# A two-layer hybrid decoder step: where products with an inverse deviation, a norm's parts and a scan's steps are emitted

## The chip, the cores and the metric

The kernel runs on one core of one Trainium2 chip, as one launch. The metric is device time in microseconds (us), lower is better; the value that counts is the median over several runs. The kernel before took 1984.57 us, the median of three runs (1982.0 to 1985.96).

The engines are TensorE (PE in the profile: matmuls, with PEld for its weight loads), VectorE (DVE, `V` in the code), ScalarE (ACT, `S`), GpSimd (POOL, `G`) and SyncE (SP, `nc.sync`), which here only issues DMAs.

## The reference

One inference step of a decoder with two layers, for a prompt of 512 tokens and 8 samples of 4 tokens (544 tokens in all, model width 1024). Per layer:

```
h = RMSNorm(x) * (1 + scale1(c)) + shift1(c)
z = h @ W_in
A: causal pooling          B: retention (4 heads), o * rsqrt(mean(o^2) + eps) * silu(gate)
C: short gated convolution D: RWKV-7, a delta-rule state, y normalised per head, bonus, output gate
mixed = sum over branches of sigmoid(gate) * (branch @ w_br);  x = x + gate1(c) * (mixed @ W_out)
h2 = RMSNorm(x) * (1 + scale2(c)) + shift2(c)
x = x + gate2(c) * W_down(silu(a) * b),   [a|b] = causal_dwconv3(h2 @ W_up)
```

A final RMSNorm gives y; each branch also returns its new state. Everything is float32.

## The kernel before, in words

**Layout and matmuls.** Activations lie transposed: channels on 128 partitions, the 544 tokens along the free dimension, split into two halves of 272 (`HS`). Every large product is done in three passes (`mm3`, L156 to L167): weight and activation are each split into a high part (rounded to float32r) and a low part (the rest), and PE runs high x high (L164), high x low (L165) and low x high (L166). `unit` (L200) does one 128-wide output tile for one half: 8 `mm3`, 24 matmuls, into one PSUM tile `pd` (three of them). Another engine evicts it. Weights come by SP's DMA; ACT rounds the high part (`whi`, L130) and DVE subtracts the low part (`wlo`, L134).

**The order is written out.** PE, DVE, ACT and POOL run their instructions in the order in which the Python code emits them; only SP's DMAs are left to a scheduler. So an instruction that waits holds up all that was emitted after it on its engine. Side work is woven between the large matmuls by a clock of matmuls: `nmm[0]` goes up by 3 in each `mm3`, which then calls `slot()` (L183). `later(n, fn)` runs `fn` once n more matmuls were emitted; a generator that was handed to `spawn` yields the number of matmuls until its next step (the sign sets the order in a slot; a `True` behind it lets another generator's matmuls go with that step). `finish(e)` runs all steps that are left at once.

**The mixer.** After eight units for branch D, `rwkv` (L459) is spawned. Meanwhile the main program does the short convolution (6 units), its gates, the pooling (2 units), its gates, the retention's 8 units, then the gates of branch D and of branch B. `gates` (L1210) does per tile of 128 channels a gate unit in both halves, which ACT's sigmoid evicts (L1247), and, one tile later, the projection (2 x 6 matmuls), evicted by DVE with a product (L1227); then POOL (L1229), in the last call DVE, adds it up. In the calls for D and B, `finish` of the generator stands behind the second gate unit.

`rwkv` makes decays and, tile of 128 tokens by tile, `products` (L528): four DVE products that go into `LG` (L544, L546), then four into `bks` (L552) and one into `bkd` (L558), which the matmuls L579 and L586 of the next step read. Then come a substitution of 31 steps on DVE, the scan of 16 chunks (G matmul L734, its copy L696, S matmul L701, its copy L705, state and output matmuls L754 and L758, state update L767 or, in the first chunk, L769), a last chunk for the samples, and a norm: Ln (L450) and Exp (L453) on ACT give the inverse deviation, with which DVE multiplies (L853 and on). `retentions` (L960) waits for the scan's end and then does `retention` for two head pairs: three steps of matmuls, Ln and Exp, and the products L954 and L955, with the split L456 (ACT) and L457 (DVE).

**The norms.** `both_halves` (L384) drives the output projection and the last part of the down projection: 8 tiles for the first half of the tokens, then 8 for the second. DVE adds each tile to x (`residual`, L408 to L415), ACT squares it (L322), DVE adds up the squares (L325). Behind each half a norm generator is spawned: a matmul with ones (L331), square root (L333), reciprocal (L355), then per tile a product (L361, DVE), scale and shift (L338, ACT, with L343 and L344 on DVE for the samples), the high part (L366, ACT) and the low part (L369, DVE). The first half's norm runs beside the second half's tiles; the second half's norm runs beside the first units of the next stage. The last norm, `norm_final`, multiplies on DVE (L379) and sends each pair of tiles out from SP's queue (L381).

Of the kernel before, what the change touches and what calls it, by code (L numbers as in the profile page):

```python
# [12 lines left out]
AF = mybir.ActivationFunctionType  # L13
ALU = mybir.AluOpType
MUL, ADD, SUB, MAX = ALU.mult, ALU.add, ALU.subtract, ALU.max
# [7 lines left out]
PAST_LEN = 4096  # L23
D_FF = 2816
NU = 138
D_G, D_S, D_P = 15, 15, 18
KAPPA = -math.exp(-0.5)

RW_UNITS = [22, 23, 18, 19, 16, 17, 20, 21]
# [14 lines left out]
def tile_hybrid_step(ctx: ExitStack, tc: tile.TileContext, io: dict):  # L44
    nc = tc.nc
    V, S, G, PE = nc.vector, nc.scalar, nc.gpsimd, nc.tensor
# [20 lines left out]
    def ZR(n=562, dt=F32):  # L67
        return zrp.tile([128, n], dt, tag="zr", name=nm("zr"))
# [109 lines left out]
    def later(n, fn):  # L178
        laters.append((nmm[0] + n, fn))
# [136 lines left out]
    def xk(xt, k):  # L316
        return xt[k // 4][:, k % 4, :]

    def sum_sq(acc, x):

        sq = ZR(x.shape[1])
        S.activation(sq, x, AF.Square)  # L322
        if acc is None:
            return sq
        later(5, lambda: V.tensor_tensor(out=acc, in0=acc, in1=sq, op=ADD))  # L325
        return acc

    def rstd_sqrt(acc):
# [21 lines left out]
    def norm_half(xt, half, acc, sA, shA, hh):  # L350

        c0, c1 = HS[half]
        rs = rstd_sqrt(acc)
        yield -8
        V.reciprocal(rs, rs)  # L355
        yield -10
        us = {}
        for i in range(11):
            if i < 8:
                us[i] = ZR(HALF)  # L360
                V.tensor_tensor(out=us[i], in0=xk(xt, i)[:, c0:c1], in1=rs, op=MUL)  # L361
            if 0 <= i - 1 < 8:
                mod_samples(us[i - 1], i - 1, half, sA, shA)
                mod_prompt(us[i - 1], i - 1, half, sA, shA)
            if 0 <= i - 2 < 8:
                S.copy(hilo_of(i - 2, half, hh)[0], us[i - 2])  # L366
            if 0 <= i - 3:
                hi, lo = hilo_of(i - 3, half, hh)
                V.tensor_tensor(out=lo, in0=us[i - 3], in1=hi, op=SUB)  # L369
            yield -8 if half == 0 else -7  # L370

    def norm_final(xt, half, acc):
        c0, c1 = HS[half]
        rs = rstd_sqrt(acc)
        V.reciprocal(rs, rs)
        yield -6
        for k in range(8):
            x = xk(xt, k)[:, c0:c1]
            V.scalar_tensor_tensor(out=x, in0=x, scalar=pars[0][:, P_FG + k:P_FG + k + 1], in1=rs, op0=MUL, op1=MUL)  # L379
            if k % 2:  # L380
                nc.sync.dma_start(io["o_y"][:, k - 1:k + 1, c0:c1], xt[k // 4][:, k % 4 - 1:k % 4 + 1, c0:c1])  # L381
            yield -6

    def both_halves(run, norm):  # L384

        ng = None
        for half in range(2):
            acc = None
            for m in range(8):
                acc = sum_sq(acc, run(m, half))  # L390
                fill()
            if ng:
                finish(ng)
            ng = spawn(norm(half, acc), 24, first=False)
        return ng
# [56 lines left out]
    def exp_half(out):  # L452
        S.activation(out[:, 0:TOK], out[:, 0:TOK], AF.Exp, scale=-0.5)  # L453
# [5 lines left out]
    def rwkv(l, za, zb, M, yD):  # L459
# [68 lines left out]
        def products(T, e1):  # L528
# [8 lines left out]
            for q in range(2):  # L537
                r = par_rows(q)
                o = LG[q][r, 4 * T:4 * T + nch, :, :]
                ot = o.rearrange("r c p t -> r p c t")  # L540
                kb = kkb[r, 0:2, t0:t0 + n].rearrange("r p (c t) -> r p c t", t=32)
                Er = E[r].rearrange("r p (c t) -> r p c t", t=32)
                oa, orr = ot[:, :, :, a_cols(q)], ot[:, :, :, r_cols(q)]
                V.tensor_tensor(out=oa[:, :, :, 1:32], in0=kb[:, :, :, 1:32], in1=Er[:, :, :, 0:31], op=MUL)  # L544
                G.tensor_copy(oa[:, :, :, 0:32:st], kb[:, :, :, 0:32:st])
                V.tensor_tensor(out=orr, in0=zb[r, 0:2, t0:t0 + n].rearrange("r p (c t) -> r p c t", t=32),  # L546
                                in1=Er, op=MUL)
            bks = ZR(512)
            bkv = bks[:, 0:4 * n].rearrange("p (q c w t) -> p q c w t", q=2, w=2, t=32)
            for w, src in enumerate((kkb, za)):  # L550
# [10 lines left out]

        e1 = decays(0)
        yield -16
        bkn = products(0, e1)
        yield 54, True
        for T in range(5):
            n = 128 if T < 4 else 32
            nch = n // 32
# [32 lines left out]
                                          LG[q][b_rows(q, p), 0:16, p, a_cols(q)])  # L601
            if T < 4:
                yield -14
                bkn = products(T + 1, e1)
                yield 50, True
        rks = []
        for p in range(2):
            rk = ZR(TOK)
# [50 lines left out]
        for s in range(31):  # L659
            substitute(s)  # L660
            if s % 2:
                yield -18, False, s > 28
        for h in range(2):
            nc.sync.dma_start(scr2[:, :, h, :], X[64 * h:64 * h + 64])
        for q in range(2):
# [180 lines left out]
            ln_bones(rs, TOK, 1.0 / 64, EPSL, rs)  # L846
        for rs in rss:
            exp_half(rs)
        yield -8
        yD.append(T4(F32R))  # L850
        for p in range(2):
            y = yv[:, p, :]
# [9 lines left out]
    def retention(l, p, rt, M, yB):  # L862
# [19 lines left out]
        for ps in pss:  # L882
# [1 line left out]
            V.tensor_tensor(out=sm.rearrange("j (T i) -> j T i", T=4), in0=ps.rearrange("j (T i) -> j T i", T=4),  # L884
                            in1=cst[:, C_RETM:C_RETM + 128].unsqueeze(1).broadcast_to([128, 4, 128]), op=MUL)
            sms.append(sm)
        yield 36, True
        ps = PM()
        pv = PM()
        for q in range(2):  # L890
# [17 lines left out]
        for T in range(1, 4):  # L908
# [4 lines left out]
        V.tensor_tensor(out=Vx[0:64].rearrange("r (b e) -> r b e", b=NB),  # L913
                        in0=vks[0:64, 0:64].unsqueeze(1).broadcast_to([64, NB, 64]),
                        in1=cst[0:64, C_BM:C_BM + 8].unsqueeze(2).broadcast_to([64, NB, 64]), op=MUL)
        yield 36, True
        psO = PM()
        for T in range(4):
            for q in range(2):
# [31 lines left out]
        rs = ZR(TOK)  # L951
        ln_bones(sq, TOK, 1.0 / 64, EPS6, rs)
        exp_half(rs)
        V.tensor_tensor(out=o, in0=o, in1=rs, op=MUL)  # L954
        V.tensor_tensor(out=o, in0=o, in1=rt[:, 3, :], op=MUL)  # L955
        if p == 0:
# [744 lines left out]
```

## Time and profile before

| | us |
|---|---|
| median of three runs | 1984.57 |
| lowest, highest | 1982.0, 1985.96 |
| the profiled execution | 1986.48 |
| its span on the core | 1984.7 |
| PE busy | 1914.8 |
| DVE busy | 1097.5 |
| ACT busy | 813.6 |
| POOL busy | 244.9 |
| mean granted clock of PE | 0.989 |

How to read the rows of the profile. A row of the order of time is "start, duration (us), engine, line, operation, output<-inputs, shape, xcount", and in brackets how long the engine sat idle before it and what ended that. A row of the list of waits is "who <- for whom: us in all, times, the longest". A row of the groups ends in "busy us, mean ns | idle us before"; a row of one source line has the shortest, median and longest duration in ns. Large matmuls overlap: a duration of 0.29 us is the time through the array, the step from one start to the next is what they cost. A row of stages gives the stretch, its length, the busy time (and number of instructions) of PE, PEld, DVE, ACT and POOL, and then PE's mean granted clock, the DMA engines' busy share and GB/s.

### The profile page before, as it was taken

The page shows a single profiled execution, that of the slowest core. Times are in us where ns is not written, and L with a number is a line of the kernel's source. Part 1 is how long each engine was busy: PE and PEld are TensorE (multiplying, and loading weights), DVE is VectorE, ACT ScalarE, POOL GpSimd, SP SyncE. Part 2 cuts the span into 40 slices and gives each one's busy share as a digit, 9 for nine tenths or more (in the row PEclk, how much of TensorE's full clock was granted, in tenths as well). Part 3 has the DMA queues.
Part 4 walks back from the last instruction along what each step waited for, and adds up shares of the span by engine and source line. Part 5 has one row for each costly group of instructions (what it writes and reads, how often), then busy time and mean ns, then how long its engine had stood idle before and what let it go on. Part 6 is the DMA issues. An engine that isn't in the chain of part 4 may idle for free.

```text
span 1984.7 us, 39086 instructions
## 1 busy us (share of the span) xinstructions
PE 1914.8 (96%) x16188; PEld 1837.4 (93%) x16188; DVE 1097.5 (55%) x2245; ACT 813.6 (41%) x1578; POOL 244.9 (12%) x687
## 2 busy tenths in 40 slices
PE   6999999989999999999989999999899999999997
PEld 5999999888999998899989999998799999999996
DVE  5475755443566552455664756555336765445565
ACT  5643323343345531434355433334424555243532
POOL 1100135311000000000101001451110000000000
PEclk9999999999999999999999999999899999999998
DMA  8223435412334268522332133242124222222221
GB/s 320 87 93 111 121 128 173 147 61 75 131 104 160 86 224 307 193 92 88 115 120 70 64 97 89 65 134 81 59 86 151 83 86 86 86 87 95 86 94 46
DMA packets 75042, 227.15 MB, mean 114 GB/s; under 512 B 20208, under 2 KB 23072, under 8 KB 73072
## 3 DMA queue, kind: packets, MB, share of 16 engines
q1 hardware_dynamic: 69872, 210.43, 31.5%
q0 software_dynamic: 4560, 13.76, 2.2%
q8 instruction: 127, 2.08, 0.4%
q10 hardware_dynamic: 432, 0.46, 0.1%
q14 instruction: 51, 0.42, 0.1%
HBM read 213.33 MB, written 9.06 MB: 112 GB/s over the span
## 4 chain that ended last, share of the span: by engine, by line
PE 88%; DVE 7%; ACT 3%; issue 1%; DMA 0%; POOL 0%; DVEq 0%; SPq 0%; ACTq 0%
PE pd L164 27%; PE pd L166 26%; PE pd L165 26%; PE pm L282 2%; DVE wlo L134 1%; PE pm L734 1%; DVE zr L325 1%; PE pm L754 1%; DVE zr L1227 1%; ACT L453 1%; PE pm L758 1%; PE pm L579 0%; PE pm L586 0%; ACT zr L322 0%; ACT zr L450 0%
## 5 line engine op out<-in xcount | busy, mean ns | idle before, releaser
L164 PE MATMUL pd<-t,whi 128*128 128x272 f32 x4104 | 1210.5, 295 | 23.7 <-DVE zr L1227 20.9
L166 PE MATMUL pd<-t,wlo 128*128 128x272 f32 x4104 | 1192.2, 291 | 2.6 <-DVE wlo L134 2.1
L165 PE MATMUL pd<-t,whi 128*128 128x272 f32 x4104 | 1186.6, 289 | 2.1 <-DVE t L369 1.7
L164 PEld LDWEIGHTS pd<-t,whi 128*128 128x128 f32 x4104 | 778.4, 190 | 57.6 <-DVE zr L1227 24.4
L165 PEld LDWEIGHTS pd<-t,whi 128*128 128x128 f32 x4104 | 780.4, 190 | 4.2 <-DVE t L369 2.1
L166 PEld LDWEIGHTS pd<-t,wlo 128*128 128x128 f32 x4104 | 778.7, 190 | 3.2 <-DVE wlo L134 2.4
L134 DVE TENSOR_TENSOR wlo<-raw,whi 128x1024 fp32r<-128x1024 f32 x256 | 320.7, 1253 | 299.6 <-ACT whi L130 297.2
L130 ACT CAST whi<-raw 128x1024 fp32r<-128x1024 f32 x258 | 270.6, 1051 | 146.6 <-PE pd L165 139.2
L1395 ACT COPY zr<-pd 128x272 f32<-128x272 f32 (+2 forms) x264 | 73.5, 314 | 241.1 <-PE pd L166 241.0
L1247 ACT ACTIVATE zr<-pd 128x272 f32<-128x272 f32 x128 | 50.6, 397 | 215.8 <-PE pd L166 215.4
L408 DVE SCALAR_TENSOR_TENSOR t<-pd,mod,t 128x272 f32<-128x272 f32 (+1 forms) x160 | 76.7, 480 | 85.8 <-PE pd L166 85.4
L1397 POOL COPY off<-zr 128x18 f32<-128x18 f32 x88 | 19.9, 226 | 645.6 <-ACT zr L1395 645.6
L1227 DVE TENSOR_TENSOR zr<-pd,zr 128x272 f32<-128x272 f32 x96 | 40.7, 436 | 79.1 <-PE pd L166 78.6
L1152 DVE SCALAR_TENSOR_TENSOR zr<-zr,par,zr 128x560 f32<-128x560 f32 x92 | 73.8, 802 | 3.2
L1151 DVE SCALAR_TENSOR_TENSOR zr<-zr,par,zr 128x560 f32<-128x560 f32 x92 | 73.2, 796 | 3.7 <-ACT zr L1148 3.6
L1229 POOL TENSOR_TENSOR t<-t,zr 128x272 f32<-128x272 f32 x64 | 57.2, 907 | 142.4 <-DVE zr L1227 136.8
L322 ACT ACTIVATE zr<-t 128x272 f32<-128x272 f32 (+1 forms) x72 | 32.4, 455 | 95.6 <-DVE t L408 55.7
L1148 ACT ACTIVATE zr<-zr,par 128x560 f32<-128x560 f32 x92 | 65.7, 766 | 10.4 <-DVE zr L1177 10.4
L164 PE MATMUL pd<-t,t 128*128 128x272 f32 x224 | 64.8, 289 | 3.4 <-DVE zs L412 3.4
L166 PE MATMUL pd<-t,t 128*128 128x272 f32 x224 | 64.5, 288 | 0.0
L165 PE MATMUL pd<-t,t 128*128 128x272 f32 x224 | 64.4, 287 | 0.0
L696 DVE COPY gs<-pm 32x64 f32<-32x64 f32 x68 | 15.2, 224 | 64.7 <-ACT gs L696 64.1
(285 smaller groups left out, 1778.3 us busy)
## 6 DMA issues: line engine op xcount, KB each, us to landing
raw<-in_wst SPq DMA_DIRECT2D x276, 512.0 KB, 3.4
t<-in_wada SPq DMA_DIRECT2D x32, 1024.0 KB, 9.1
raw<-in_wada SPq DMA_DIRECT2D x24, 512.0 KB, 3.6
zr<-in_rope POOLq DMA_DIRECT2D x16, 272.0 KB, 4.2
t<-in_wada SPq DMA_DIRECT2D x8, 512.0 KB, 6.8
t<-in_xT SPq DMA_DIRECT2D x4, 544.0 KB, 6.2
zr<-zr POOLq DMA_DIRECT2D x32, 68.0 KB, 2.0
t<-in_xT SPq DMA_DIRECT2D x2, 1088.0 KB, 8.9
```

What stands on the lines that cost most here:

```text
L130: S.copy(hi, raw)
L134: (G if (l, u) in ((0, 1), (0, 2)) else V).tensor_tensor(out=lo, in0=raw, in1=hi, op=SUB)
L164: PE.matmul(ps, lhsT=a, rhs=xh, start=first, stop=False)
L165: PE.matmul(ps, lhsT=a, rhs=xl, start=False, stop=False)
L166: PE.matmul(ps, lhsT=b, rhs=xh, start=False, stop=last)
L408: V.scalar_tensor_tensor(out=x[:, c0:c0 + npc], in0=ps[:, :npc], scalar=gate[:, m, 0:1], in1=x[:, c0:c0 + npc], op0=MUL, op1=ADD)
L1148: S.activation(cv, u[:, 0:560], AF.Copy, scale=wcol(0))
L1151: V.scalar_tensor_tensor(out=cv, in0=u[:, 1:561], scalar=wcol(1), in1=cv, op0=MUL, op1=ADD)
L1152: V.scalar_tensor_tensor(out=cv, in0=u[:, 2:562], scalar=wcol(2), in1=cv, op0=MUL, op1=ADD)
L1227: V.tensor_tensor(out=a[:, c0:c1] if first else gs, in0=pp[:, :HALF], in1=gs, op=MUL)
L1229: (V if last else G).tensor_tensor(out=a[:, c0:c1], in0=a[:, c0:c1], in1=gs, op=ADD)
L1395: pad_evac(lambda o, i, sl: S.copy(o, i), u, ps, half, 2)
```

## The change

- The state products of a tile come in two pieces: a yield stands between the `LG` products and the `bks` products, and the yields behind them are shorter.
- The scan's third yield in each chunk (`D_P`) goes from 18 to 15; the substitution's from 18 to 16.
- Between Exp and the products with the inverse deviation stand 24 instead of 8 matmuls in `rwkv`, and 30 instead of none in `retention`. Two yields of `retention` grow from 36 to 46 and 50.
- In the second half of `both_halves`, the sums of squares of the tiles 1 to 5 go to GpSimd (the first tile has no sum, the last two stay on DVE). In the first half's norm, the low parts go to GpSimd. The yields of the norm become 9 (8 before) and 6 (7 before).
- In the last norm, two of eight tiles are scaled by ACT and multiplied by GpSimd. Each tile gets a DMA of its own, on ACT's queue and SP's in turn.

```diff
-D_G, D_S, D_P = 15, 15, 18
+D_G, D_S, D_P = 15, 15, 15
...
-    def sum_sq(acc, x):
+    def sum_sq(acc, x, eng=V):
...
-        later(5, lambda: V.tensor_tensor(out=acc, in0=acc, in1=sq, op=ADD))
+        later(5, lambda: eng.tensor_tensor(out=acc, in0=acc, in1=sq, op=ADD))
...
-                V.tensor_tensor(out=lo, in0=us[i - 3], in1=hi, op=SUB)
-            yield -8 if half == 0 else -7
+                (V if half else G).tensor_tensor(out=lo, in0=us[i - 3], in1=hi, op=SUB)
+            yield -9 if half == 0 else -6
...
-            V.scalar_tensor_tensor(out=x, in0=x, scalar=pars[0][:, P_FG + k:P_FG + k + 1], in1=rs, op0=MUL, op1=MUL)
-            if k % 2:
-                nc.sync.dma_start(io["o_y"][:, k - 1:k + 1, c0:c1], xt[k // 4][:, k % 4 - 1:k % 4 + 1, c0:c1])
+            if k % 4 == 3:
+                S.activation(x, x, AF.Copy, scale=pars[0][:, P_FG + k:P_FG + k + 1])
+                G.tensor_tensor(out=x, in0=x, in1=rs, op=MUL)
+            else:
+                V.scalar_tensor_tensor(out=x, in0=x, scalar=pars[0][:, P_FG + k:P_FG + k + 1], in1=rs, op0=MUL, op1=MUL)
+            (nc.sync if k % 2 else S).dma_start(io["o_y"][:, k:k + 1, c0:c1], xt[k // 4][:, k % 4:k % 4 + 1, c0:c1])
...
-                acc = sum_sq(acc, run(m, half))
+                acc = sum_sq(acc, run(m, half), G if half and m < 6 else V)
...
                 V.tensor_tensor(out=orr, in0=zb[r, 0:2, t0:t0 + n].rearrange("r p (c t) -> r p c t", t=32),
                                 in1=Er, op=MUL)
+            yield -14
             bks = ZR(512)
...
-        bkn = products(0, e1)
-        yield 54, True
+        bkn = yield from products(0, e1)
+        yield 46, True
...
-                bkn = products(T + 1, e1)
-                yield 50, True
+                bkn = yield from products(T + 1, e1)
+                yield 40, True
...
-                yield -18, False, s > 28
+                yield -16, False, s > 28
...
             exp_half(rs)
-        yield -8
+        yield -24
...
             sms.append(sm)
-        yield 36, True
+        yield 46, True
...
-        yield 36, True
+        yield 50, True
...
         exp_half(rs)
+        yield -30
         V.tensor_tensor(out=o, in0=o, in1=rs, op=MUL)
```

## The prediction

> **What bounds the kernel now.** The page comes first, then the waits of TensorE (PE), then the order of time on PE and on the engine that each wait names.
>
> ```profile
> span 1984.7 us, 39086 instructions
> PE 1914.8 (96%) x16188; PEld 1837.4 (93%) x16188; DVE 1097.5 (55%) x2245; ACT 813.6 (41%) x1578; POOL 244.9 (12%) x687
> ```
>
> PE is busy 96% of the span; the change removes no matmul, so it can only win what PE waits for, or what PE loses in clock. The waits of PE:
>
> ```profile
> PE pd L164 <- DVE zr L1227: 20.9, 16, 4.1
> PE pm L331 <- DVE zr L325: 16.8, 3, 12.4
> PE pd L164 <- DVE zs L412: 4.0, 4, 1.7
> PE pm L926 <- DVE t L907: 3.6, 2, 1.8
> PE pm L734 <- DVE z L769: 1.8, 2, 1.2
> PE pm L579 <- DVE zr L558: 1.8, 2, 0.9
> PE pd L165 <- DVE t L369: 1.7, 2, 1.3
> ```
>
> Every wait is for DVE, an engine that is busy 55%: it is not full, it is blocked in order. Where the largest ones sit, on PE (first two rows: the first and the last of 15 undisturbed matmuls), then DVE, then ACT:
>
> ```profile
> 379.73 0.29 PE L164 MATMUL pd<-t,whi 128*128 128x272 f32 x1
> 381.50 0.29 PE L166 MATMUL pd<-t,wlo 128*128 128x272 f32 x1
> 422.86 0.39 PE L164 MATMUL pd<-t,whi 128*128 128x272 f32 x1 [1.63 <-DVE zr L1227]
> 427.20 0.59 PE L164 MATMUL pd<-t,whi 128*128 128x272 f32 x1 [2.57 <-DVE zr L1227]
> 427.59 0.43 PE L165 MATMUL pd<-t,whi 128*128 128x272 f32 x1
> 430.31 0.39 PE L165 MATMUL pd<-t,whi 128*128 128x272 f32 x1
> 454.26 0.48 PE L164 MATMUL pd<-t,whi 128*128 128x272 f32 x1 [4.11 <-DVE zr L1227]
> 1406.31 0.40 PE L164 MATMUL pd<-t,whi 128*128 128x272 f32 x1 [2.56 <-DVE zr L1227]
> 1433.44 0.39 PE L164 MATMUL pd<-t,whi 128*128 128x272 f32 x1 [4.11 <-DVE zr L1227]
> ```
>
> ```profile
> 398.60 0.73 DVE L853 TENSOR_TENSOR t<-t,zr 128x544 f32<-128x544 f32 x1 [5.50 <-ACT zr L453]
> 419.53 0.73 DVE L954 TENSOR_TENSOR t<-t,zr 128x544 f32<-128x544 f32 x1 [8.08 <-ACT zr L453]
> 422.37 0.43 DVE L1227 TENSOR_TENSOR zr<-pd,zr 128x272 f32<-128x272 f32 x1
> 450.94 0.73 DVE L954 TENSOR_TENSOR t<-t,zr 128x544 f32<-128x544 f32 x1 [8.33 <-ACT zr L453]
> 453.77 0.43 DVE L1227 TENSOR_TENSOR zr<-pd,zr 128x272 f32<-128x272 f32 x1
> ```
>
> ```profile
> 446.77 1.28 ACT L450 ACT_TABLE_LOAD   x1 [1.55 <-PE pm L445]
> 450.25 0.66 ACT L453 ACTIVATE zr<-zr 128x544 f32<-128x544 f32 x1
> 454.41 0.40 ACT L1247 ACTIVATE zr<-pd 128x272 f32<-128x272 f32 x1
> ```
>
> L954 stands in the DVE queue right behind the emission of Ln and Exp, so DVE idles (8.33 us) until Exp ends at 450.91; the eviction L1227, whose data lay ready in PSUM, runs only at 453.77, and PE starts 0.06 us after that ends. The same happens at 419.53, and in the second layer at the same places (1406.31, 1433.44).
>
> A second loss stands behind each stall. Undisturbed, 14 steps take 381.50 - 379.73 = 1.77 us, 0.126 us each; after the stall, 12 steps take 430.31 - 427.59 = 2.72 us, 0.227 us each. That stretch costs 12 x 0.10 = 1.2 us beside its stall. The granted clock says so too:
>
> ```profile
> 420.00:460.00 40.00, 31.69 (x283) 29.38 (x282) 15.80 (x28) 17.70 (x27) 8.60 (x11) 0.91 0.17 54
> ```
>
> 0.91 is the mean granted clock there. The Trainium skill ("TensorE: Matmul & The Clock Gate", Part 1) has the array drop to half clock only after an idle window of about 3.4 us. By that rule only the two 4.11-us stalls would bring a half-clock stretch (rival e below). The half-clock stretch after the 2.57-us wait speaks against it; I keep the row.
>
> **The change part by part.** The kernel's own clock counts matmuls in threes, so a step falls due at the next multiple of 3: 18 to 16, and 8 to 9 in the first half's norm, change nothing (cost 0, nothing moves). I count positions from the spawn of the rwkv generator. The products take 18+15+48 in place of 18+54 before the first tile and 15+15+42 in place of 15+51 before the other four: +33. Sixteen chunks at 45 in place of 48: -48. The scan so ends at 1719 instead of 1734, its norm's Ln/Exp stand at 1761 instead of 1776, and its products, 24 instead of 9 behind, at 1785 as before. The retentions start at 1722 instead of 1740; their steps fall at 1740, 1788, 1839, 1875 (Ln/Exp), 1905 (products), the second ones at 2058 and 2088. The forced finishes stand at 1824 and 2304, so nothing is forced.
>
> Term 1, the products behind Exp. Exp ends 450.91, about 4.1 us after PE's L445 released the table load at 446.77. Thirty matmuls give 30 x 0.126 = 3.8 us, and the two L445 matmuls that are issued first add some; DVE then meets a finished Exp within about half a microsecond. L1227, queued ahead of the products, gets through. The wait of L926 goes too: DVE waited 5.50 us at 398.60 for its Exp, and 15 more matmuls (1.9 us) lie between Ln and products, 9 more (1.1 us) between products and L926. The six long L1227 waits (1.63 + 2.57 + 4.11 = 8.3, and as much in the second layer, whose 2.56 and 4.11 are above: 16.6 of the 20.9) and L926's 3.6 are 20.2 us. What is late next is ACT: the copy L456 still waits for L955 and the gates' sigmoids stand behind it. I take 18.5; bounds 12 (the 427.20 kind stays in both layers, and some of L926) and 20.2.
>
> Term 2, the half-clock stretches behind six stalls (three a layer), 1.2 each: 7.2. I take 6.5; bounds 2.4 and 7.2.
>
> Term 3, products in two pieces and the shorter scan. The DVE work before the first tile's L579 is the same, PE comes 9 matmuls (1.1 us) later: its 0.9 twice goes. Scan start moves 33 matmuls (4 us) away from the pooling sums that held L769 (1.8). Against it, each chunk has 3 matmuls (0.38 us) less to hide its state update. The tightest chunk I found:
>
> ```profile
> 1259.58 0.61 DVE L767 TENSOR_TENSOR z<-pm,pt 64x128 f32<-64x128 f32 x2
> 1260.61 0.61 PE L734 MATMUL pm<-z,t 128*128 128x128 f32 x4
> ```
>
> 1260.61 - 1260.19 = 0.42 us, just over 0.38, and the new phases (45 against the gates' 60) differ. The moved steps' DMAs (state loads and stores on POOL's queue, the scratch round trip on SP's) keep their distance to their readers. I take +3; bounds -2 and +3.6.
>
> Term 4, the norm shared with GpSimd. It matters between the layers, where DVE falls behind PE: 4.0 (L412) + 1.7 (L369) + 1.2 (L331: 16.8 less 12.4 at the start and 3.2 at the end) = 6.9 us. In that stage:
>
> ```profile
> L369 DVE TENSOR_TENSOR t<-zr,t 128x272 fp32r<-128x272 f32 x8 | 3.5, 434 | 0.0
> DVE zr L325 <- ACT zr L322: 4.1, 8, 0.6
> L1229 POOL TENSOR_TENSOR t<-t,zr x64: 753/770/1757, 256.8 to 1462.5; 128x272 f32<-128x272 f32 x64
> 1283.31 0.76 POOL L1229 TENSOR_TENSOR t<-t,zr 128x272 f32<-128x272 f32 x1 [0.92 <-DVE zr L1227]
> 1283.34 1.82 DVE L134 TENSOR_TENSOR wlo<-raw,whi 128x1024 fp32r<-128x1024 f32 x1 [0.17 <-ACT whi L130]
> L134 DVE TENSOR_TENSOR wlo<-raw,whi x256: 1160/1226/1832, 27.4 to 1933.9; 128x1024 fp32r<-128x1024 f32 x128
> L1227 DVE TENSOR_TENSOR zr<-pd,zr x96: 424/434/444, 256.2 to 1523.3; 128x272 f32<-128x272 f32 x96
> ```
>
> Off DVE go 8 low parts (3.5 us) and 5 sums with the wait before each (5 x (0.43 + 4.1/8) = 4.7, a sum being as long as a low part): 8.2 us of its queue. On to POOL come 13 operations at 0.77: 10.0 us. POOL's and DVE's operations on SBUF shut each other out: L134, 1.23 us alone, took 1.82 when POOL started 0.03 us before it, which is nearly POOL's whole length on top. If every POOL operation did that, DVE would stand 10.0 - 8.2 = 1.8 us worse; if none did, all 6.9 come back. But L408 and L412 take one input from PSUM, as L1227 does, and L1227 never lasted over 0.444 in a stage that it shares with POOL's L1229. I take 2.5; bounds -2 and 6.9. The other two norm stages show no wait of this kind, cost 0 while DVE keeps up. The second half's norm at 6 in place of 9 only hands DVE its work earlier.
>
> The Trainium skill ("SBUF — State Buffer", Who interferes with whom) calls this an exclusive lock between a DVE operation with two SBUF inputs and a GpSimd operation that reads SBUF. The trace agrees (1.82 against 1.23). By the rule taken strictly, this term is -1.8.
>
> Term 5, the end.
>
> ```profile
> 1971.62 0.46 DVE L408 SCALAR_TENSOR_TENSOR t<-pd,mod,t 128x240 f32<-128x240 f32 x1
> 1973.46 1.27 PE L331 MATMUL pm<-zr,cst 128*128 128x272 f32 x2 [3.20 <-DVE zr L325]
> 1977.18 3.39 DVE L379 SCALAR_TENSOR_TENSOR t<-t,par,zr 128x272 f32<-128x272 f32 x8
> 1978.12 2.85 SPq L381 DMA_DIRECT2D o_y<-t  x4
> ```
>
> PE was done at 1973.46 - 3.20 = 1970.26, DVE began the last tile at 1971.62: 1.36 us of backlog from sums that wait for squares. On POOL those no longer block: +1.3. The last products get longer: six on DVE end at 6 x 0.42 = 2.5 after the start; the last tile's scale on ACT stands behind an output DMA that waits for the sixth, so a DMA issue (four took 2.85 with the gaps between them: under 0.7, I take 0.4), a scale (0.4, my estimate from L453's 0.66 on twice the elements) and POOL's 0.77 follow: 4.1, with DVE and POOL shutting each other out 4.9, against 3.39. A last transfer half as large gives a little back. I take -0.8, so +0.5; bounds -1.3 and +1.4.
>
> Sum: 18.5 + 6.5 + 3 + 2.5 + 0.5 = 31.0. The profiled execution took 1986.48 (span 1984.7 and 1.8 around it), so it becomes 1955.5. The median of the runs stands 1.9 below it at 1984.57: 1953.6.
>
> **The rivals.** (a) ACT takes the wait over. Behind Exp, L456 waits for the moved products, and the next sigmoid needs another table (1.28 as above). If that holds PE as at 427.20, in two to four places, 2.57 + 1.2 each, 7.5 to 15 come back: about 1965. For it: ACT's chain isn't shortened. Against: at 454.26 PE went on before the late sigmoid of 454.41 had run, so its bank is wanted later than L1227's. (b) DVE and POOL shutting each other out decides the norm stages: term 4 at -1.8, and the two norm stages after the mixers lose as much: 1953.6 + (2.5 + 1.8) + 2 x 1.8 = 1961.5. For it: the 1.82 row. Against: DVE gets 8.2 us off. (c) Slower: the scan's chain becomes the bound. If DVE's weight subtraction at its locked length (1.82) stood before the state update in each of the 32 chunks, with 0.42 - 0.38 of slack left, each would stall 1.78: 57 us, 2008. It decides against the change from (31 + 4) / 32 = 1.1 us a chunk. Against: only two scan steps wait for the update now. (d) The change does nothing: the evictions find other work before them and each stall forms again in its new place: 1984.6. Against: 8 us of DVE idle before L954 is there to be filled. (e) The half-clock stretches are bound to the 4.11-us stalls alone and the others stay, having another cause: term 2 is 2 x 1.2 = 2.4, and the time 1957.7. For it: 4.11 is the longest idle. Against: the stretch at 427.59.
>
> **How the numbers follow.** Forecast 0.65, (a) 0.12, (b) 0.10, (c) 0.04, (d) 0.04, (e) 0.05. A measurement of this kernel tells about 0.2% (4 us) from nothing. Faster 0.92 (forecast, a, b, e), same 0.04, slower 0.04. The terms' bounds sum to 9.1 and 39.3, 1975 and 1945; all low together is unlikely. The range 1945 to 1968 holds most of the forecast's chance with (a), (b) and (e).
>
> **What would show it.** Right: PE's list without L1227 waits over 1 us and without L926; L954's idle before it ended by something else than L453; granted clock 1.00 where 0.91 stood; no L579 and no L734 wait over 0.5; L412 and L369 waits under half, with POOL's new operations longer than 0.77 in part. Wrong: PE waiting for ACT L1247 (a), for POOL's low parts or L408 in the stages after the mixers (b), for L767 in most chunks (c).

## The result and the profile after

The kernel after takes 1953.24 us, the median of four runs (1952.54 to 1955.75); the kernel before, run beside it, takes 1985.26 (1982.0 to 1988.78). The ratio is 0.9841 (95% interval 0.9821 to 0.986): 32 us faster, where 31.0 were forecast. The profiled execution took 1952.54 us, with a mean granted clock of 0.993.

In the kernel after, the lines from the last norm's products on stand three to five further down: L412 is now L415, L453 is L456, L579 is L583, L734 is L738, L926 is L930, L954 is L959, L1227 is L1232 and L1247 is L1252. The page of the kernel after:

```profile
span 1950.4 us, 39168 instructions
PE 1900.2 (97%) x16188; PEld 1825.1 (94%) x16188; DVE 1093.0 (56%) x2197; ACT 819.8 (42%) x1586; POOL 287.9 (15%) x735
```

PE has as many instructions as before and ends 34.3 us of span earlier (1984.7 - 1950.4), so all of the gain is time in which PE waited or ran slowly. POOL has 43 us more work (287.9 - 244.9). The waits of PE, kernel after:

```profile
PE pm L331 <- DVE zr L325: 15.1, 3, 12.7
...
PE pm L804 <- POOL z L800: 4.1, 2, 2.1
PE pd L164 <- DVE zr L1232: 3.6, 10, 0.6
PE pd L164 <- ACT zr L1252: 2.6, 2, 1.3
...
PE pm L705 <- issue: 1.4, 1, 1.4
PE pd L165 <- POOL t L369: 1.3, 2, 1.0
PE pd L164 <- DVE zs L415: 0.6, 1, 0.6
...
PE pm L583 <- DVE zr L562: 0.2, 1, 0.2
```

The 20.9 us for the projection's eviction have become 3.6, with no wait over 0.6 us; L926's 3.6 are gone. Two waits are new: L804 for a clearing on POOL (4.1), and the gates' sigmoid on ACT (2.6). A third has grown: the scan's S matmul L705 (L701 in the kernel before) now waits 1.9 us in all, at the first chunk, where it waited 0.6. From 420 to 460 us and from 1400 to 1440 us the granted clock was 0.91 in the kernel before; in the kernel after:

```profile
420.00:460.00 40.00, 38.54 (x361) 36.12 (x361) 18.17 (x28) 19.41 (x30) 6.99 (x10) 1.00 0.21 68
1400.00:1440.00 40.00, 37.98 (x310) 36.26 (x309) 14.46 (x19) 16.19 (x25) 8.11 (x10) 1.00 0.29 94
```

The order of time on DVE, kernel after, at the two places of the first layer where L954 had waited 8.08 and 8.33 us:

```profile
416.48 1.19 DVE L1232 TENSOR_TENSOR zr<-pd,zr 128x272 f32<-128x272 f32 x3
418.84 1.13 DVE L959 TENSOR_TENSOR t<-t,zr 128x544 f32<-128x544 f32 x1 [1.17 <-ACT zr L456]
...
453.47 0.43 DVE L1232 TENSOR_TENSOR zr<-pd,zr 128x272 f32<-128x272 f32 x1
453.82 0.71 DVE L959 TENSOR_TENSOR t<-t,zr 128x544 f32<-128x544 f32 x1
```

The evictions L1232 now run ahead of the product; it meets Exp finished (second place) or 1.17 us early (first). That is step one of the forecast, seen directly.

**Where the time came from.** Both kernels run the same 13248 large matmuls (L164 to L166) in the same order, so the time from one of them to another can be compared. From the retention's first unit to the gates of branch B, layer 0 takes 12.5 us less and layer 1 11.0 less: 23.5. Everything from rwkv's start to there: 0.9 and 1.8, together 2.7. Between the layers 4.7, at the end 3.1; at the start 0.25 are lost ahead of the first large matmul and 0.3 are won behind it; elsewhere under 0.1 each. The border between the first two groups isn't sharp, as the scan's small matmuls move across it.

One trace of each kernel stands behind such numbers, and stretches in which nothing was edited differ between traces too: from the first large matmul to rwkv's start, the kernel before takes 62.9 us here, and two other kernels with the same instructions up to there take 65.0. A difference of one or two us in one stretch says little unless other traces repeat it. Of the 4.7 us between the layers, the 2.7 in the last part of layer 0's down projection are repeated by the five other traces in which both the sums and the low parts are shared with GpSimd. The other 2.0, in the first units of layer 1, are 0.4 to 2.0 there.

### The profile page after: what moved, and what is told of

It reads as the page before. It is cut to its first block, busy times and chain, and to the rows that moved or that the text cites. A ratio compares the mean times of both kernels' runs of the same rounds, so it can differ in the third digit from the quotient of the medians.

```text
span 1950.4 us, 39168 instructions
## 1 busy us (share of the span) xinstructions
PE 1900.2 (97%) x16188; PEld 1825.1 (94%) x16188; DVE 1093.0 (56%) x2197; ACT 819.8 (42%) x1586; POOL 287.9 (15%) x735
## 4 chain that ended last, share of the span: by engine, by line
PE 91%; DVE 4%; ACT 3%; issue 1%; DMA 1%; POOL 0%; SPq 0%; POOLq 0%; DVEq 0%; ACTq 0%
PE pd L164 27%; PE pd L166 27%; PE pd L165 26%; PE pm L282 2%; DVE wlo L134 1%; ACT whi L130 1%; PE pm L738 1%; PE pm L758 1%; PE pm L762 1%; PE pm L583 0%; DVE zr L1232 0%; PE pm L448 0%; DMA t<-in_xT 0%; PE pm L590 0%; PE pm L705 0%
## 5 line engine op out<-in xcount | busy, mean ns | idle before, releaser
L164 PE MATMUL pd<-t,whi 128*128 128x272 f32 x4104 | 1205.2, 294 | 8.9 <-DVE zr L1232 3.6
L166 PE MATMUL pd<-t,wlo 128*128 128x272 f32 x4104 | 1187.9, 289 | 2.6 <-DVE wlo L134 2.1
L164 PEld LDWEIGHTS pd<-t,whi 128*128 128x128 f32 x4104 | 773.4, 188 | 42.0 <-issue 21.9
L166 PEld LDWEIGHTS pd<-t,wlo 128*128 128x128 f32 x4104 | 773.8, 189 | 3.2 <-DVE wlo L134 2.4
L134 DVE TENSOR_TENSOR wlo<-raw,whi 128x1024 fp32r<-128x1024 f32 x256 | 319.1, 1247 | 317.1 <-ACT whi L130 316.1
L1252 ACT ACTIVATE zr<-pd 128x272 f32<-128x272 f32 x128 | 50.4, 397 | 210.0 <-PE pd L166 198.7
L1232 DVE TENSOR_TENSOR zr<-pd,zr 128x272 f32<-128x272 f32 x96 | 41.1, 436 | 95.6 <-PE pd L166 95.1
L325 POOL TENSOR_TENSOR zr<-zr,zr 128x272 f32<-128x272 f32 x20 | 23.0, 1149 | 288.8 <-issue 183.4
L164 PE MATMUL pd<-t,t 128*128 128x272 f32 x224 | 64.7, 289 | 0.8 <-DVE zs L415 0.6
L166 PE MATMUL pd<-t,t 128*128 128x272 f32 x224 | 64.6, 288 | 0.0
```

Source lines behind the costliest of these rows:

```text
L134: (G if (l, u) in ((0, 1), (0, 2)) else V).tensor_tensor(out=lo, in0=raw, in1=hi, op=SUB)
L164: PE.matmul(ps, lhsT=a, rhs=xh, start=first, stop=False)
L166: PE.matmul(ps, lhsT=b, rhs=xh, start=False, stop=last)
L1252: S.activation(gs, ps[:, :HALF], AF.Sigmoid)
```

## The experiments

The theory behind the forecast: PE loses time to instructions that stand, on an in-order engine, behind another one that waits; what helps is distance between the wait and what it holds up. Its rivals: ACT's chain is the bound, and the moved products only move the wait; the shorter scan starts to hold PE; the sharing with GpSimd costs as much as it gives; the gain comes from another part than the moved products. Times are medians of the runs. The kernel before took 1986.44, 1983.97 and 1984.14 us beside the three groups of experiments.

### The moved products alone

Against the kernel before:

```diff
             exp_half(rs)
-        yield -8
+        yield -24
...
             sms.append(sm)
-        yield 36, True
+        yield 46, True
...
-        yield 36, True
+        yield 50, True
...
         exp_half(rs)
+        yield -30
```

> The kernel before with only the four yields around Ln and Exp of the change (24 in the scan's norm; 46, 50 and the new 30 in the retention); all else as before. Theory A (DVE's queue was blocked by products that waited for Exp, and PE lost its clock behind the stalls): the stretch from the retention units to the second gates shortens by 22 to 26 us, PE's waits for L1227 fall from 20.9 to under 5 us and the one of L926 goes, time 1958 to 1963. Theory B (DVE was short of time, and GpSimd's share is what helped): under 5 us less, 1980 or more.

Measured: 1965.43 us, ratio 0.9893 (0.9872 to 0.9913). PE's waits:

```profile
PE pd L164 <- ACT zr L1248: 6.4, 2, 3.2
PE pd L164 <- DVE zr L1228: 4.1, 10, 0.9
```

L1227's 20.9 (one line lower here) are 4.1 and L926 is gone, as expected; but the rival with ACT comes up as well, 6.4 us. Where, on PE and ACT:

```profile
1378.61 0.59 PE L164 MATMUL pd<-t,whi 128*128 128x272 f32 x1 [3.22 <-ACT zr L1248]
```

```profile
1377.61 0.65 ACT L456 CAST t<-t 128x544 fp32r<-128x544 f32 x1 [2.10 <-DVE t L857]
1378.16 0.39 ACT L1248 ACTIVATE zr<-pd 128x272 f32<-128x272 f32 x1
```

It isn't the table load here: ACT sits idle for 2.10 us ahead of the copy L456, which waits for rwkv's moved product L857, and the sigmoid that PE needs stands behind that copy. It is the same mechanism one engine on. In the whole change the wait is down to 2.6 us. From the retention's first unit to the gates of branch B, the two layers together take 23.0 us less, inside the expected 22 to 26. The time as a whole lies between the two expected ranges: in this trace, 3.5 us are lost at the start and between the layers, where nothing was edited.

### The change without its two moves behind Exp

Against the kernel after:

```diff
             exp_half(rs)
-        yield -24
+        yield -8
...
         exp_half(rs)
-        yield -30
```

> The changed kernel with the products right behind Exp again (8 in the scan's norm, none in the retention; the 46 and 50 stay). Theory A: the waits for the projection's eviction come back in both layers with the half-clock stretches, 18 to 25 us, time 1971 to 1978. Theory B: 1953 to 1957.

Measured: 1974.77 us, ratio to the kernel before 0.9935 (0.9913 to 0.9958), so 0.0094 of 1985, or 19 us, of the whole change's gain is lost. PE's list has the old wait again:

```profile
PE pd L164 <- DVE zr L1231: 15.8, 14, 4.3
```

So the moved products carry about six tenths of the change's 32 us, from both sides: 21.0 us when they are moved alone (1986.44 - 1965.43, with the two longer yields), 19 lost when the two moves are left out.

### The norm shared with GpSimd, alone

Against the kernel before:

```diff
-    def sum_sq(acc, x):
+    def sum_sq(acc, x, eng=V):
...
-        later(5, lambda: V.tensor_tensor(out=acc, in0=acc, in1=sq, op=ADD))
+        later(5, lambda: eng.tensor_tensor(out=acc, in0=acc, in1=sq, op=ADD))
...
-                V.tensor_tensor(out=lo, in0=us[i - 3], in1=hi, op=SUB)
-            yield -8 if half == 0 else -7
+                (V if half else G).tensor_tensor(out=lo, in0=us[i - 3], in1=hi, op=SUB)
+            yield -9 if half == 0 else -6
...
-                acc = sum_sq(acc, run(m, half))
+                acc = sum_sq(acc, run(m, half), G if half and m < 6 else V)
```

> The kernel before with only the norm's share for GpSimd (five sums a norm, the first half's low parts, yields 9 and 6). Theory A (the wait of the sums for the squares leaves DVE's queue, the lock between DVE and GpSimd gives part of it back): 4 to 5 us less between the layers and 1.5 to 2 us less before the last norm, time 1978 to 1980. Theory L (the lock takes all): 1985 or more. In both, DVE's L361 lasts up to 1.0 us beside GpSimd, against 0.43.

Measured: 1979.99 us, ratio 0.9966 (0.9955 to 0.9976). Between the same matmuls, 3.3 us come back between the layers (4 to 5 were expected) and 2.8 at the end (1.5 to 2 expected).

### The last norm on three engines, alone

Against the kernel before (the branch for ACT and GpSimd and the DMA for each tile, as in the diff of the change):

```diff
+            if k % 4 == 3:
+                S.activation(x, x, AF.Copy, scale=pars[0][:, P_FG + k:P_FG + k + 1])
+                G.tensor_tensor(out=x, in0=x, in1=rs, op=MUL)
+            else:
+                V.scalar_tensor_tensor(out=x, in0=x, scalar=pars[0][:, P_FG + k:P_FG + k + 1], in1=rs, op0=MUL, op1=MUL)
```

> The kernel before with only the last norm on three engines and a DMA for each tile. My prediction's step says 0.8 us slower; the trace of the changed kernel says that the last issue comes 1 us later and the smaller transfer lands 1.1 us sooner, so no difference: 1984.5 to 1986, last output issue about 4.3 us after the first product against 3.4 before.

Measured: 1986.21 us, ratio 1.0002 (0.9992 to 1.0012): no difference in the time. In its one trace the end is 1.2 us shorter all the same, and PE's idle of 0.45 us beside the last tiles is gone; 2.0 us more stand at the start of that trace, where nothing was edited.

### The products in two pieces and the shorter scan, alone

Against the kernel before:

```diff
-D_G, D_S, D_P = 15, 15, 18
+D_G, D_S, D_P = 15, 15, 15
...
+            yield -14
             bks = ZR(512)
...
-        bkn = products(0, e1)
-        yield 54, True
+        bkn = yield from products(0, e1)
+        yield 46, True
...
-                bkn = products(T + 1, e1)
-                yield 50, True
+                bkn = yield from products(T + 1, e1)
+                yield 40, True
```

> The kernel before with only the products in two pieces and the scan at 45 matmuls a chunk (the retention's yields as before). Theory A (the predicted step): L579's and L734's waits of 0.9 and 0.7 to 1.2 go, 2.5 to 3.5 us less in the two stretches, no new wait in the scan's middle; against it a new wait of about 2.1 us a layer for POOL's clearing of the last chunk's rows, as in the changed kernel, so the sum is near zero: 1982 to 1987. Theory C (the scan's chain becomes the bound): PE waits for the state update L767 in most chunks, 1995 or more.

Measured: 1977.2 us, ratio 0.9964 (0.9951 to 0.9977): faster than expected. PE's waits:

```profile
PE pd L164 <- DVE zr L1228: 11.6, 14, 2.6
PE pm L801 <- POOL z L797: 4.1, 2, 2.1
```

No wait for the state update in the chunks: the rival with the scan's chain falls. The waits at L579 and L734 are gone, as forecast. But two things were not expected. The evictions' wait falls from 20.9 to 11.6, though nothing moved between Exp and its product: the retentions start 18 matmuls earlier, and their product meets other evictions behind it. And the clearing's wait of 4.1 us comes from this part.

### Only another phase

If what counts is which eviction is queued behind the waiting product, then shifting both retentions should help, with no distance added between Exp and its product.

```diff
-        yield 18, True
+        yield 51, True
```

The kernel is that of before; the line stands ahead of the first of the two calls of `retention`.

> The kernel before with one number changed: the retention's first yield is 51 instead of 18, so that its Ln, Exp and products, still in one step, fall at 1899 and 2025 (before: 1866 and 1992), just behind a projection's last eviction instead of just ahead of the next. Theory A (the Exp wait costs only what is queued behind it on DVE within PE's slack): L1227's waits fall from 20.9 to under 8 us and the half-clock stretches of the retention go, 1963 to 1970; L926's wait stays. Theory S (products must stand apart from Exp, wherever they are): no gain, 1982 to 1988.

Measured: 1962.13 us, ratio 0.9892 (0.9877 to 0.9907). One number gives 22 us, as much as the four yields of the first experiment. Two details were expected otherwise: L1227's waits are 8.9 and not under 8, and L926's wait, which was to stay, has gone, as the retention's matmuls now come later too. PE's wait, and DVE's order of time:

```profile
PE pd L164 <- DVE zr L1227: 8.9, 14, 1.8
```

```profile
417.97 1.12 DVE L1227 TENSOR_TENSOR zr<-pd,zr 128x272 f32<-128x272 f32 x3
422.55 0.73 DVE L954 TENSOR_TENSOR t<-t,zr 128x544 f32<-128x544 f32 x1 [3.45 <-ACT zr L453]
```

L954 is still emitted straight behind Exp and still idles DVE for 3.45 us; but the evictions went ahead of it, and PE needs nothing of DVE in that time. So Exp's latency alone doesn't make the stall; what stands in the queue behind the product does. Distance still helps: in the first experiment the evictions' waits were 4.1 in place of 8.9.

### The clearing: on another engine, and earlier

The wait of L804 for L800 in the kernel after, on POOL and then PE:

```profile
366.11 2.02 POOL L1343 DMA_DIRECT2D zr<-zr  x4 [0.87 <-ACT zr L1334]
368.12 0.57 POOL L797 DMA_DIRECT2D o_wkv_p<-pn  x1
368.68 0.48 POOL L800 MEMSET z<- 64x128 f32 x2
```

```profile
368.96 0.49 PE L804 MATMUL pm<-z,t 128*128 128x128 f32 x2 [2.06 <-POOL z L800]
```

The clearing takes 0.48 us and waits for nothing; but on POOL's queue stand four DMA issues ahead of it, and those wait for ACT. In the kernel before the queue is the same:

```profile
367.07 2.02 POOL L1338 DMA_DIRECT2D zr<-zr  x4 [6.18 <-ACT zr L1329]
...
369.64 0.48 POOL L796 MEMSET z<- 64x128 f32 x2
```

But there the clearing's reader, 15 matmuls later in the order, starts at 371.07, and nothing waits. The shorter scan brings the reader ahead of the clearing. First remedy, the clearing on DVE, against the kernel after:

```diff
-            G.memset(Z[q][par_rows(q), 0], 0.0)
+            V.memset(Z[q][par_rows(q), 0], 0.0)
```

> The changed kernel with the clearing of the last chunk's state rows (before the samples' chunk) on DVE instead of POOL. Theory A (that clearing stands in POOL's queue behind DMA issues that wait for an eviction by ACT, and PE waits for it since the scan ends earlier): PE's wait of 4.1 us goes, and with it up to 1.4 us of half clock: 1947.5 to 1949.5 . Rival (another chain ends just as late, such as the input of the samples): under 1 us less, 1952 to 1954.

Measured: 1953.74 us, ratio to the kernel before 0.985 (0.9827 to 0.9873), no difference from the kernel after. PE's wait was for the most part moved rather than removed (`L804 <- DVE z L800`, 2.8 us in place of 4.1), since DVE's queue is held there too:

```profile
368.13 1.22 DVE L134 TENSOR_TENSOR wlo<-raw,whi 128x1024 fp32r<-128x1024 f32 x1 [1.55 <-ACT whi L130]
369.32 0.41 DVE L800 MEMSET z<- 64x128 f32 x2
```

Second remedy, the same clearing on POOL but earlier, where its block is made, against the kernel after:

```diff
                 Zn = newZ([(vT, 0), (vT, 1)] if T < 3 else [(vT, 3)])
+                if T == 3:
+                    for q in range(2):
+                        G.memset(Zn[q][par_rows(q), 0], 0.0)
...
-        for q in range(2):
-            G.memset(Z[q][par_rows(q), 0], 0.0)
```

> The changed kernel with the clearing of the last chunk's state rows moved ahead, on POOL, to where the block is made (two chunks earlier). Theory A (what stood ahead of the clearing in its queue made PE wait, on POOL as on DVE): the 4.1 us of waits go with no heir over 1 us, 1947 to 1950. Rival (the rotation's transfers hold the last chunk anyway): 1952 to 1954.

Measured: 1946.89 us, ratio 0.9815 (0.9798 to 0.9832). On POOL and PE:

```profile
351.06 0.46 POOL L755 MEMSET z<- 64x128 f32 x2
```

```profile
367.53 0.38 PE L805 MATMUL pm<-z,t 128*128 128x128 f32 x2
```

The clearing is done 16 us before its reader, and PE waits no more. The retention's stretches (up to its last unit) get 2.3 and 3.8 us shorter than in the kernel after: the two stalls of 2.06 and 2.05, and in the second layer the 1.39 us that PE had lost at half clock behind its stall. These are 5.5 of the 6.1.

### The sums of squares back on DVE, and a GpSimd that only writes

Against the kernel after:

```diff
-                acc = sum_sq(acc, run(m, half), G if half and m < 6 else V)
+                acc = sum_sq(acc, run(m, half), V)
```

> The changed kernel with all sums of squares on DVE; the first half's low parts stay on GpSimd. Theory A (what helped was above all that DVE no longer waits for the squares): the 4.7 us between the layers and the 3.1 at the end come back in large part, 1957 to 1960. Rival (the low parts alone unload DVE enough): 1953 to 1955.

Measured: 1960.53 us, ratio 0.9882 (0.9862 to 0.9901). Between the same matmuls, 2.45 us are lost between the layers and 1.9 at the end, so in the whole change the sums on GpSimd carry 4.3 of the 7.8 us that these two places gave. Of the 2.45, 2.1 lie in the down projection's last part, whose 2.7 other traces repeat. The time is half a us above the expected range. To price what the two engines cost each other, the low parts of this kernel were then replaced by three writes of zeros on POOL, in one profiled execution:

```diff
-                (V if half else G).tensor_tensor(out=lo, in0=us[i - 3], in1=hi, op=SUB)
+                if half:
+                    V.tensor_tensor(out=lo, in0=us[i - 3], in1=hi, op=SUB)
+                else:
+                    for _ in range(3):
+                        G.memset(lo.bitcast(F32), 0.0)
```

> As the one with all sums on DVE, but in place of each low part of the first half GpSimd writes zeros to it three times: the low parts aren't computed, GpSimd works about as long and reads nothing. If reading is what shuts DVE out: DVE's L361 between the layers lasts 0.43 throughout and L134 1.23. If any work of GpSimd on SBUF does: L361 reaches 0.7 to 1.0 as with the real low parts.

Measured: 1959.92 us. DVE's product L361 in the kernel after, with the low parts alone on POOL, and with the writes (shortest, median and longest in ns):

```profile
L361 DVE TENSOR_TENSOR zr<-t,zr x48: 428/434/1048, 560.4 to 1553.6; 128x272 f32<-128x272 f32 x48
```

```profile
L361 DVE TENSOR_TENSOR zr<-t,zr x48: 428/434/1023, 563.4 to 1558.8; 128x272 f32<-128x272 f32 x48
```

```profile
L361 DVE TENSOR_TENSOR zr<-t,zr x48: 426/434/440, 562.5 to 1558.3; 128x272 f32<-128x272 f32 x48
```

Beside POOL's subtractions and sums, a product of DVE takes up to 1.05 us in place of 0.43. The third row alone doesn't say that POOL must read for that: the writes wait for nothing, so POOL ran them in one block ahead of each norm, and none of them fell beside an L361. Inside such a block, however, DVE ran other operations with two inputs from SBUF:

```profile
526.15 8.31 POOL L373 MEMSET t<- 128x272 f32 x24 [53.35 <-PE pd L166]
```

```profile
529.22 1.22 DVE L134 TENSOR_TENSOR wlo<-raw,whi 128x1024 fp32r<-128x1024 f32 x1
531.18 0.43 DVE L464 TENSOR_TENSOR t<-t,t 128x272 fp32r<-128x272 f32 x1
```

Both are as short as elsewhere (medians 1.225 and 0.436), so a POOL that only wrote did not shut DVE out. In the time as a whole it hardly counts: without the low parts the kernel took 1959.92 in one execution, against a median of 1960.53.

### The version that the experiments point to

To the earlier clearing were added: the last norm's eight products on DVE again, with a DMA for each tile; and 27 matmuls in place of 18 before the second retention, to let ACT's sigmoid go ahead.

```diff
-            if k % 4 == 3:
-                S.activation(x, x, AF.Copy, scale=pars[0][:, P_FG + k:P_FG + k + 1])
-                G.tensor_tensor(out=x, in0=x, in1=rs, op=MUL)
-            else:
-                V.scalar_tensor_tensor(out=x, in0=x, scalar=pars[0][:, P_FG + k:P_FG + k + 1], in1=rs, op0=MUL, op1=MUL)
+            V.scalar_tensor_tensor(out=x, in0=x, scalar=pars[0][:, P_FG + k:P_FG + k + 1], in1=rs, op0=MUL, op1=MUL)
...
-        yield 18, True
+        yield 27, True
```

> The changed kernel with three edits: the clearing ahead as above; the last norm's eight products on DVE with the DMAs of the change; the second retention 9 matmuls later, so that its Ln stands behind, not ahead of, the gate's sigmoid. From the traces: 4.1 us and up to 1.4 of half clock for the first, about 0.9 us for the second (the last issue 3.4 instead of 4.4 us after the first product, the smaller transfer kept), 2.6 us for the third (PE's waits for ACT's sigmoid): 1943.5 to 1947.

Measured: 1945.46 us, ratio 0.9806 (0.9791 to 0.982), the fastest of all. PE's wait for the sigmoid has fallen from 2.6:

```profile
PE pd L164 <- ACT zr L1249: 0.7, 2, 0.3
```

Against the kernel with the earlier clearing, and between the same matmuls, 1.5 us come back in the gates of each layer and 0.3 at the end; 1.6 are lost between the layers, where nothing was edited. The intervals of the two ratios overlap, so what the last two edits add to the clearing is not settled. Every run of both versions (1949.36 at most) is shorter than every run of the kernel after (1952.54 at least).

## Why the prediction was right, step by step

| Step | forecast, us | measured in the spans, us |
|---|---|---|
| products behind Exp, and the half-clock stretches (terms 1 and 2) | 18.5 + 6.5 | 23.5 |
| products in two pieces, shorter scan (term 3) | 3 | 2.7, and in the first row the new wait of L804 |
| norm shared with GpSimd, between the layers (term 4) | 2.5 | 4.7 |
| the end (term 5) | 0.5 | 3.1 |
| start | 0 | 0.1 |
| elsewhere | 0 | 0.2 |
| sum | 31.0 | 34.3 (span), 32.0 (medians) |

**Terms 1 and 2 held, with a cost inside them that was not foreseen.** From the lists of waits: 17.3 us of L1227's and 3.6 of L926's wait went, a little more than term 1's upper bound of 20.2; 2.6 for the sigmoid and 4.1 for the clearing came. 17.3 + 3.6 - 2.6 - 4.1 = 14.2, against 18.5. The half clock gave more than forecast. Summed over all steps between neighbouring large matmuls of 0.19 to 0.26 us, what lies above 0.126 is 31.1 us in the trace of before and 22.3 in that of after. Of these 8.8, 8.1 lie in the stretches of the 23.5, against a forecast of 6.5. 14.2 + 8.1 = 22.3; the remaining 1.2 are not assigned. The size of one half-clock stretch was the error: the six behind the stalls, taken at 1.2 each, measure 1.3 to 1.9, together 9.0. All six are gone, and a new one of 1.39 stands behind L804. The rival by which the half-clock stretches hang on the 4.11-us stalls alone has fallen: in both gate windows the clock is 1.00.

The reason given for term 1 was half of the truth. It said that distance makes Exp ready. The run with another phase shows that Exp may stay late; the evictions must be ahead of the product. The same two places of the kernel after show both: one product waits 1.17 us still, and PE does not notice.

**The step that failed: "The moved steps' DMAs (state loads and stores on POOL's queue, the scratch round trip on SP's) keep their distance to their readers."** The forecast looked at the DMAs of the moved steps and not at the clearing that shares POOL's queue with them, nor at the retention's DMA issues (L1338, in the kernel after L1343) that hold that queue until ACT is done; the reader came 15 matmuls earlier, and what POOL's queue waits for did not. It cost 4.1 us of waits and 1.39 of half clock, 6.1 us in all by the stretches that the earlier clearing shortened. That the total came so close is luck: the waits of the table's first row gave 4.3 less than term 1 forecast, this cost among the reasons, and terms 2, 4 and 5 were too low by 6.4 together (1.6 + 2.2 + 2.6).

**Term 3** held in what it named: L579's 1.8 became 0.2 (up to 1.1 in other traces with the same edit), L734's wait is gone, no chunk waits for its state update. Against it stands L705's wait, 1.9 in place of 0.6, which the sum had not counted.

**Term 4 was too small, inside its bounds.** DVE and POOL do shut each other out, both ways: L361 takes up to 1.05 us, and POOL's sums 0.77 to 1.76, where the median of POOL's L1229 on as many elements is 0.77 (shortest, median and longest in ns, kernel after):

```profile
L325 POOL TENSOR_TENSOR zr<-zr,zr x20: 766/1073/1759, 562.2 to 1935.5; 128x272 f32<-128x272 f32 x20
```

The Trainium skill ("SBUF — State Buffer", Who interferes with whom) has this lock for a DVE operation with two SBUF inputs against a GpSimd operation that reads SBUF, and not against one that only writes; this case agrees on both, by the rows of L361 in the kernel after (up to 1.05) and those of L134 and L464 inside the block of writes (1.22 and 0.43). But the strict reading of it, -1.8, had the wrong sign: DVE's busy time alone doesn't decide. A sum of squares that waits for ACT held all that stood behind it in DVE's queue; on POOL less that is urgent stands behind it, and taking the sums back to DVE lost 2.45 of the 4.7. Part of the 4.7 varies from trace to trace; each trace with the shared norm wins at least 3.1 between the layers, which is nearer to the forecast of 2.5.

**Term 5 was mis-sized, and outside its bounds (-1.3 to 1.4).** The end, kernel after, in order of time:

```profile
1939.87 0.73 PE L331 MATMUL pm<-zr,cst 128*128 128x272 f32 x2 [1.82 <-DVE zr L325]
...
1943.04 2.56 DVE L383 SCALAR_TENSOR_TENSOR t<-t,par,zr 128x272 f32<-128x272 f32 x6
1946.02 0.52 ACT L380 ACTIVATE t<-t,par 128x272 f32<-128x272 f32 x1 [0.71 <-DVE t L383]
1946.62 0.76 POOL L381 TENSOR_TENSOR t<-t,zr 128x272 f32<-128x272 f32 x1 [0.40 <-ACT t L380]
1947.41 0.33 SPq L384 DMA_DIRECT2D o_y<-t  x1
```

POOL's last product ends at 1946.62 + 0.76 = 1947.38, and SP issues its DMA at 1947.41, 4.37 us behind the first product, inside the forecast's 4.1 to 4.9. But the last transfer is half as large, and the rows on the landing of the output DMAs, of the kernel before (pairs of tiles) and of the kernel after (single tiles), say what that gives:

```profile
DMA to landing us min/median/max: 2.2/2.4/2.9
```

```profile
DMA to landing us min/median/max: 1.7/1.8/2.0
```

The last transfer of all landed 2.83 us after its issue in the first (1980.60 to 1983.43) and 1.73 in the second (1947.41 to 1949.14). From first product to landing that is 3.42 + 2.83 = 6.25 against 4.37 + 1.73 = 6.10: the -0.8 became +0.15. That the last norm alone makes no difference to the time (1.0002) agrees. The rest has two parts. L331's wait fell from 3.20 to 1.82 and its own time from 1.27 to 0.73; this goes with the sums, for the shared norm alone gives 2.8 us at the end too, and with the sums back on DVE 1.9 of the 3.1 are lost again. And PE's idle of 0.45 us at 1965.53 in the kernel before, which cost 0.6 with the step behind it, has no counterpart; it is gone with the shared norm alone, with the last norm alone, and with the sums back on DVE, so either edit removes it.

**The other rivals.** ACT took over a wait, but 2.6 us where 7.5 to 15 were allowed for. The norm stages after the mixers differ by less than 0.1 us, so GpSimd's share costs nothing there. Two slips in the prediction change nothing in its sum: "every wait is for DVE" holds for the rows that it shows, but PE's list has 3.6 us for ACT (L258) too, at the start of the kernel; and 1953.6 + 57 is 2010.6, not 2008. Two of the signs that were named did not come: one of L959's waits is still ended by Exp, and the wait of the low part L369 fell from 1.7 only to 1.3, now for POOL.

## What to carry to other kernels

When an engine is half idle and yet others wait for it, read what stands behind its idle instruction in its queue: an instruction that waits can be given distance, or be put right behind the last one that somebody needs, and each gave 21 to 22 us here. When a step is moved, go through every queue that it issues to, and look at what waits ahead of even its cheapest instruction: a clearing of 0.48 us cost 6 us. That wait was cured by emitting the clearing earlier; handing it to another engine only asked which queue was less blocked.

## What the runs showed of the hardware that was not expected

**Half clock without a long idle, and not each time.** The same wait of L804 stands in both layers of the kernel after. PE behind it, first layer and then second:

```profile
370.08 0.29 PE L165 MATMUL pd<-t,whi 128*128 128x272 f32 x1
370.20 0.28 PE L166 MATMUL pd<-t,wlo 128*128 128x272 f32 x1
...
1314.83 2.04 PE L790 MATMUL pm<-t,zr 64*64 64x8 f32 x64
1316.79 0.42 PE L164 MATMUL pd<-t,whi 128*128 128x272 f32 x1
1317.02 0.42 PE L165 MATMUL pd<-t,whi 128*128 128x272 f32 x1
...
1329.77 0.49 PE L804 MATMUL pm<-z,t 128*128 128x128 f32 x2 [2.05 <-POOL z L800]
1331.07 0.43 PE L165 MATMUL pd<-t,whi 128*128 128x272 f32 x1
1331.30 0.43 PE L166 MATMUL pd<-t,wlo 128*128 128x272 f32 x1
```

Behind the first wait of 2.06 us the steps are 0.12 us, behind the second of 2.05 they are 0.23; and at 1316.79 the half clock comes with no stall at all, behind 64 matmuls of 8 columns. In the kernel before, such a stretch stands behind these 64 matmuls in both layers, in the kernel after in the second alone. The Trainium skill ("TensorE: Matmul & The Clock Gate", Part 1) says that the gate looks at a free-running window, which would let the same stall count once and not the other time; that fits. Its figure of about 3.4 us of idle before the drop does not: the 2.57-us stall in the trace of before was followed by such a stretch too. What decides for one stall stays open; so the stretch behind a stall is a chance and not a certainty.
